# Taking the elementwise work off GpSimd in a two-layer recurrent and convolutional backbone

## The chip, the cores and the metric

The kernel runs on one core of a Trainium2 chip. The metric is the device time of one execution in microseconds. Within the core, TensorE does the matrix products, VectorE, ScalarE and GpSimd the elementwise work, and SyncE (SP) issues the DMAs. The engines run side by side and wait for one another by semaphores; each takes its own instructions strictly in the order of its program. In the profile they are PE (with PEld for its weight loads), DVE, ACT, POOL and SP.

## The reference

Two layers over 1024 latent tokens of 1024 channels, with a context of 256 tokens that goes through the first mixer alone. All is float32. Cut to what is computed:

```python
for l in range(2):
    sm, cm, gm, sf, cf, gf = split(silu(c) @ ada_w[l] + ada_b[l], 6)     # modulation, also of c_ctx
    hl = rms_norm(x, norm_mix_g[l]) * (1 + cm) + sm
    if l == 0:      # bidirectional RG-LRU, the context in front of the latents in each direction
        u = conv(hl @ w_x)                             # width 4, and the same for the context
        r, i = sigmoid(u @ w_r + b_r), sigmoid(u @ w_i + b_i)     # by heads of 256 channels
        a = exp(8 * r * log_sigmoid(lam)); b = sqrt(1 - a * a) * i * u
        h = scan(a, b) forward + scan(a, b) backward
        y = (gelu(hl @ w_gate) * h) @ w_out
    else:           # short gated convolution
        b, g, v = split(hl @ w_in, 3); y = (b * conv3(g * v)) @ w_out
    x = x + gm * y
    hl = rms_norm(x, norm_ffn_g[l]) * (1 + cf) + sf
    g, v = split(hl @ w_up, 2)
    x = x + gf * ((silu(conv3(g)) * v) @ w_down)
return rms_norm(x, final_g)
```

## The kernel before

Channels lie on the 128 partitions, tokens along the free axis, so a tensor of 1024 channels is eight tiles of 128 x 1024. Every product is made of three products in a shorter format: each operand is split into a high part (hi, rounded to fp32r) and a low part (the source minus hi), and hi x hi, hi x lo and lo x hi go into the same PSUM bank (`mm`, line 436). `split` (line 231) makes the parts: the high one on ScalarE, or on the engine that it is given, the low one always on VectorE.

The stages of the first 455 us, around which the change lies, in order:

The start (`start`, line 567). Per tile k of x: load x and a column block of the modulation weights; `dot` (line 314) makes one modulation column as the sum of a row-wise product of 1024 columns (on VectorE one instruction with an accumulator; on GpSimd a product, and then a pass of ScalarE that sums it); the weights scaled by it are split (tiles wh/wl of the code, bh and bl in the trace), x is split (uh, ul), squared by ScalarE and added to a running sum of squares (`add(acc, acc, q, ...)`, line 625; acct in the trace), and TensorE runs 18 products. Then the norm is made, and for the second part of the start (lines 651 to 665, from about 53 us) per tile k another modulation column comes (`late_dot`), x is scaled by VectorE (x<-x,cols,cs), split (bh, bl), and 18 products run for each k. Beside that come columns for the context (`ctx_dot`, against ccb).

Then gates and products of latents and context, the norm of the context (`ctx_rstd`, line 696, sums of squares in cs6), and the small chain of 16 columns that makes the softplus (line 524; sp in the trace).

The recurrence (`ri`, line 779), eight blocks of 128 channels. Per block and direction TensorE makes two gates; ScalarE takes them out of PSUM with tanh (mx<-banks), makes the coefficients (mx<-mx,sp), VectorE multiplies and scans (TENSOR_TENSOR_SCAN), and both directions are added and multiplied with the gate. Seven slots of the tile mx hold what is under way. Between the blocks run products for the inputs u, their split (`u_split`, line 727; uh, ul), and modulation columns for later (acct<-acct,cb). At its end `ysplit` (line 857) splits the result (bh, bl). In this stage the weights' high part (wh<-raw) is made by GpSimd: `weight_hi[0] = G` (line 776) stands until `open_ffn` sets it to None.

The weights come through three tiles raw0 and six half-slots (wh, wl). A slot is free when TensorE has run the unit that last used it, so the instruction that makes wh waits for TensorE. PSUM has four banks that take turns (`bank`).

From about 455 us on come the output projection, the feed-forward part, the second layer; there GpSimd has nothing.

The order of the instructions is made by `Plan` (line 52): all instructions are recorded, then every engine gets its list ahead of time. TensorE keeps the program's order; the others take, by a cost per engine and size (`cost`, line 102), what could run next and is due first for TensorE. In these costs an add of 1024 columns is 1.15 us on VectorE and 2.30 us on GpSimd, a high part of 1024 columns 0.96 us on ScalarE and 1.01 us on GpSimd. `weight_item` (line 325), `block_items` (line 335) and `run_units` (line 369) bring the stream of loads and splits into the units.

Of the kernel before, what the change touches and what calls it, by code (L numbers as in the profile page):

```python
# [15 lines left out]
KD = 8  # L16
# [8 lines left out]
# one column per 128 channels of every per-channel vector  # L25
# [10 lines left out]
# the seven products of a 2 x 2 block product, in the order in which they run: the bank each goes to,  # L36
# whether it starts it, and its operand among the blocks of the inputs
# [3 lines left out]
# the products of the modulation of the context beside each step of the start's second part  # L41
DOTS = (0, 0, 0, 1, 1, 2, 2, 2)
# the units of the first mixer after its start: gates, products of the latents and of the context, blocks of the
# recurrence, and columns of the modulation
ORDER = ("g2 shift g3 norm g4 g5 ctx mx us0 e6 x4 r0 d3 x5 d2 r1 d2 us2 x6 d1 r2 d1 x7 d1 r3 d1 us4 d1 r4 d1 g6 r5 "
         "us6 g7 r6 r7")
# the functions that the table serves which comes with a function
# [4 lines left out]
class Plan:  # L52
    """Records the instructions and gives every engine its order ahead of time. The tensor engine keeps the program's
    order; the others take, among what could run next, the instruction that the tensor engine needs first."""
# [11 lines left out]
    def record(self, engine, op, a, k):  # L66
# [19 lines left out]
        if func:  # L86
            # those that share a table may pass each other
            if TABLE[func] != self.table[0]:
                self.table = TABLE[func], self.table[2], []
            preds.update(self.table[1])  # L90
            self.table[2].append(i)
# [9 lines left out]
    @staticmethod  # L101
    def cost(engine, op, a, k):
        """How long the engine is held"""
        if engine == "sync":
            return 4 * int(np.prod(a[0].shape)) / 360e3
        n = max(int(np.prod(v.shape[1:])) for v in list(a) + list(k.values()) if isinstance(v, bass.AP))
        if engine == "tensor":
            n = a[2].shape[-1]
            return max(n, 128) / 2400 * (4 if a[2].dtype == F32 else 1)
        if engine == "scalar":  # L110
            return 0.09 + n * 0.85e-3 + (0.09 if "accum_out" in k else 0)
        if engine == "gpsimd":
            return 0.15 + n * (2.1e-3 if op == "tensor_tensor" else 0.84e-3)
        return 0.07 + n * (6.25e-3 if op == "reciprocal" else 1.05e-3)

    @staticmethod
    def lag(a, b):
        """From the end of an instruction to the start of one that waits for it"""
        return 0.0 if a == b else 0.95 if a == "sync" else 1.9 if b == "sync" else 0.2

    def flush(self):
# [9 lines left out]
        # the latest start that keeps the tensor engine going  # L131
# [52 lines left out]
def hybrid_kernel(ctx: ExitStack, tc: tile.TileContext, out, xs, cs, c, cc, ada, vecs,  # L184
# [18 lines left out]
    def ring(name, n):  # L203
        """The next of n slots that take turns"""
        turn[name] = turn.get(name, -1) + 1
        return turn[name] % n
# [67 lines left out]
    units = []  # L274
# [11 lines left out]
    class Raw:  # L286
        """A load in the stream into one of the tiles of a pool, and the items that still need it"""
# [3 lines left out]
    class Item:  # L291
        """An entry of the stream: prep(slots, raws) makes the operand that the key stands for"""
# [21 lines left out]
    def dot(dst, raw, bt, eng=None):  # L314
        """dst = the sums of raw * bt along the rows"""
# [19 lines left out]
    def block_items(name, src1, src2, again):  # L335
        """The seven operands that two tiles of weights give: A11 A12 are the halves of the first, A21 A22 those
        of the second"""
# [31 lines left out]
    def run_units(nside):  # L369
        """Emit the units in order. What they need comes ahead as slots allow, with nside(key) modulation chunks  # L370
        behind each weight."""
# [64 lines left out]
    def mm(ps, w, wi, rh, rl, start, stop, **o):  # L436
        """ps += w[:, wi].T @ (rh + rl), both operands in two exact parts"""
# [29 lines left out]
    def norm_quick(acc, n, dg, ps=None, more=None):  # L467
        """1 / sqrt(mean + eps) per token, on all partitions: the sums with the tokens on the partitions, then
        spread from a diagonal (products with ones and zeros)"""
# [17 lines left out]
    # cols: per norm an A (8) and a B (8)  # L487
# [4 lines left out]
    def make_ab(i, src, l, sh, sc, gname, k=None):  # L492
        """A = g (1 + scale), B = shift, from the products of the modulation without its bias (in vec with the 1
        added for the scales)"""
# [23 lines left out]
    # ================= start =================  # L518
    # softplus(-lam): max(-lam, 0) + log1p(exp(-|lam|)), the log1p as 2 atanh(z / (2 + z))
# [23 lines left out]
    # ================= layer 0 mixer: RG-LRU =================  # L543
# [23 lines left out]
    def start():  # L567
        """The first products run as the data arrives, before the norm is known: with A = g (1 + scale),
        z = W.T (A x r + B) = ((A W).T x) r + W.T B"""
        A, B = ab(0)  # L570
        NM = 3
        # memory that is not in use yet
# [23 lines left out]
        # the tensor engine runs at its full clock only when it is kept busy; a bank that is not in use yet  # L596
# [7 lines left out]
        for k in range(KD):  # L604
# [19 lines left out]
            if k:  # L624
                add(acc, acc, q, G if k < 6 else V)
# [16 lines left out]
        # the next three tiles, from the norm itself as it comes  # L642
# [8 lines left out]
        for k in range(KD):  # L651
            late_dot(k, G)
# [43 lines left out]
    def ctx_rstd():  # L696
        acc, r = cs6[:, 0], cs6[:, 1]
        act(acc, xc[:, 0], AF.Square)
        for k in range(1, KD):
            q = cs6[:, 2 + k % 4]  # L700
            act(q, xc[:, k], AF.Square)
            add(acc, q, acc, G)
# [15 lines left out]
    def conv_a(z, u, m):  # L718
        """z (psum) -> u: width 4, two to the left, one to the right"""
# [7 lines left out]
    def u_split(m):  # L727
        uh[m], ul[m] = uht[:, m % 2], ult[:, m % 2]
        split(uh[m][:, ALL], ul[m][:, ALL], u32[m], G)
        split(uh[m][:, CT], ul[m][:, CT], uc[:, m], G)  # L730
# [41 lines left out]
    def open_mx():  # L772
# [3 lines left out]
        weight_hi[0] = G  # L776
        tpool[0] = lambda n: mxp[0][:, ring("mx", NMX), :n]

    def ri(m):
        """Both directions of one block of 128 channels: gates, coefficients and scans"""  # L780
        hd, mo = m // 2, m % 2

        def f(*ws):
            st = []
            # the slots in the order in which the block before lets go of them
# [3 lines left out]
            for d in range(2):  # L789
                q = d * 8 + m  # L790
                # the scan takes the context first: it stands left of the latents forward, right of them backward
# [16 lines left out]
                # sigmoid(z) = (1 + tanh(z / 2)) / 2, the halves of the biases in vec  # L808
# [13 lines left out]
            # 1 - a^2 = tanh(-log(a) / 2) (1 + a)^2  # L822
# [11 lines left out]
            for d, (q, lat, ct, R, il, ic, I) in enumerate(st):  # L834
# [5 lines left out]
                else:  # L840
                    rev = slice(None, None, -1)
                    mul(ic, ic, Tn[:, ct], G)
# [6 lines left out]
            if m in gt:  # L849
                add(fw, fw, bw, G)  # L850
                mul(x[:, m], gt[m], fw)
            else:
                add(x[:, m], fw, bw, G)
# [3 lines left out]
    def ysplit(h, ms):  # L857
        for m in ms:
            split(hhi[m][:, H[h]], hlo[m][:, H[h]], x[:, m, H[h]], G if m < 6 else None)
            load_x(m, H[h])  # L860

    side += [(ada[0, o + k], modc[:, o + k:o + k + 1], ccb, V if o else G) for k in range(KD) for o in (0, 8)]
    mods = [mod_item(0, j) for j in range(16, 48)] + [mod_item(1, j) for j in range(48)]

    def ahead_dots(todo, room=None):
        """Modulation of later parts, as time allows"""
# [44 lines left out]
    def open_ffn():  # L911
# [10 lines left out]
        # where stored inputs land while no sums are in the way  # L922
        more["stage"] = [flat(more["s"], i, 2) for i in (0, 2, 4)]
        # snapshots of sums, sums of weights, and what the norms need
# [7 lines left out]
    def block_norm(i, slots):  # L932
        """slots: 28 in the order in which they come free. The input of the products is A (x r) + B, in halves of
        the channels (first digit) and of the tokens (second); T1 to T4 are the sums that block products take."""
# [30 lines left out]
        def sums():  # L965
            # in the bank that the last of the first four units takes
# [33 lines left out]
    def blocks(name, src1, src2, post, early=False):  # L1000
        """256 output channels for all tokens from the blocks of the norm: seven products of blocks in place of
        eight. post(row, half, a, b) takes a sum a + b, or b alone."""
# [45 lines left out]
    def run_blocks(us, second, n, skip):  # L1048
        """The first four units begin with what needs only the first half of the tokens. n columns of the modulation
        come beside the products"""  # L1050
# [25 lines left out]
    def act_items(l, n, slots, h, afters, load_after, src, direct=()):  # L1076
        """The stored inputs of the next products, two tiles of 128 channels at a time"""
# [19 lines left out]
    # ================= layer 0 mixer, output =================  # L1097
# [7 lines left out]
    def out_proj(i, l, keys, yh, yl, slots, cols_args, early=()):  # L1105
        """early: tiles and halves that go together, the last input of all of them last, as it may come late"""
# [48 lines left out]
    # ================= FFN =================  # L1155
    def ffn(l, second, i):
# [36 lines left out]
        def store_blocks(q, a, b):  # L1193
            """Two tiles as the blocks that the second product takes: tokens in halves, a above b"""
# [19 lines left out]
    def act_item(key, src, load_after, slots, after, pool="raw"):  # L1214
        """A stored input of products, two tiles of 128 channels"""
# [5 lines left out]
    def down(l, ends, i):  # L1221
        """The second product: blocks for the first 16 tiles of its inputs, in two groups, then the
        other six"""
# [53 lines left out]
    def down_blocks(l, g, q, role):  # L1277
        """x += gate * (products of blocks) for 256 channels, each sum as soon as it stands in its bank"""
# [119 lines left out]
def _tiles(w):  # L1398
    """(1024, M) -> (M / 128, 128, 1024): per 128 output channels a tile with the inputs on the partitions"""
# [46 lines left out]
```

## Time and profile before

| | |
|---|---|
| median of three runs | 2135.06 us (2134.78 to 2135.86) |
| span of the profiled execution | 2134.5 us |
| TensorE busy | 2047.5 us, 96%, 9218 products |
| VectorE busy | 1809.7 us, 85%, 2564 instructions |
| ScalarE busy | 1033.5 us, 48%, 1561 instructions |
| GpSimd busy | 173.1 us, 8%, 93 instructions |
| DMA | 307.05 MB, mean 144 GB/s |

A busy share is a mean over stages that differ. The table says of the whole that TensorE has 87 us without work; where they lie, a view by windows tells. An instruction's duration in the trace is the time that it holds its engine, and that can include waiting for something other than a semaphore, which no list of waits shows: to see it, one compares the durations of the same form (same operation, same tiles, same shape) at different times.

### The profile page before, as it was taken

What the parts mean: (1) busy time and instruction counts of PE and PEld (TensorE: products, weight loads), DVE (VectorE), ACT (ScalarE), POOL (GpSimd) and SP (SyncE); (2) the same over time, 40 slices, a digit from 0 to 9 for tenths busy, and PEclk for the clock granted to TensorE, in tenths of its full rate; (3) what the DMA queues carried; (4) which work ended last, traced back from release to release, by engine and by line L of the source; (5) the groups of instructions that cost most, each with busy time, mean ns of one, the idle gap of its engine ahead of it and who ended that gap; (6) DMA issues with size and microseconds to landing.
All of it is one profiled execution on the core that took longest, in us unless ns stands there. A gap on an engine that the chain in (4) does not pass through costs nothing.

```text
span 2134.5 us, 25093 instructions
## 1 busy us (share of the span) xinstructions
PE 2047.5 (96%) x9218; PEld 1689.4 (79%) x9218; DVE 1809.7 (85%) x2564; ACT 1033.5 (48%) x1561; POOL 173.1 (8%) x93
## 2 busy tenths in 40 slices
PE   7789889699999999999999999999999999999998
PEld 5579767588788888878888788888888888888888
DVE  7988899978998989788868988867988878688867
ACT  4564666525654344454335533434654444454345
POOL 4620335310000000000000000000000000000000
PEclk9999989899999999999999999999999999999999
DMA  7455122353233545474354144673233343364345
GB/s 261 159 175 188 40 87 72 99 186 110 89 114 123 178 163 173 157 236 146 114 166 140 54 155 165 222 242 111 71 119 129 122 151 131 109 216 160 127 131 165
DMA packets 103418, 307.05 MB, mean 144 GB/s; under 512 B 10368, under 2 KB 14720, under 8 KB 103168
## 3 DMA queue, kind: packets, MB, share of 16 engines
q1 hardware_dynamic: 103296, 305.46, 43.7%
q8 instruction: 72, 1.18, 0.2%
q14 instruction: 50, 0.41, 0.1%
HBM read 248.80 MB, written 56.62 MB: 143 GB/s over the span
## 4 chain that ended last, share of the span: by engine, by line
PE 82%; DVE 8%; issue 2%; ACT 1%; DMA 0%; POOL 0%; DVEq 0%; ACTq 0%
PE banks L165 82%; DVE mx L165 2%; DVE x L165 2%; DVE bl L165 1%; DVE wl L165 1%; DVE u L165 1%; DVE acct L165 1%; DVE sp L165 0%; DVE ul L165 0%; ACT mx L165 0%; DMA s<-bd 0%; DVE uc L165 0%; DMA acct<-in_ada 0%; ACT wh L165 0%; DVE s L165 0%
## 5 line engine op out<-in xcount | busy, mean ns | idle before, releaser
L165 PE MATMUL banks<-bl,wh 128*128 128x512 f32 (+1 forms) x2720 | 1053.8, 387 | 14.3 <-DVE bl L165 14.2
L165 PE MATMUL banks<-bh,wl 128*128 128x512 f32 (+1 forms) x2720 | 1053.8, 387 | 14.2 <-DVE wl L165 14.1
L165 PE MATMUL banks<-bh,wh 128*128 128x512 f32 (+1 forms) x2720 | 1056.8, 389 | 5.0 <-ACT bh L165 3.0
L165 PEld LDWEIGHTS banks<-bl,wh 128*128 128x128 f32 x2720 | 513.3, 189 | 125.6 <-DVE bl L165 21.8
L165 PEld LDWEIGHTS banks<-bh,wl 128*128 128x128 f32 x2720 | 513.3, 189 | 121.2 <-DVE wl L165 19.3
L165 PEld LDWEIGHTS banks<-bh,wh 128*128 128x128 f32 x2720 | 513.3, 189 | 111.7 <-ACT bh L165 4.7
L165 ACT ACTIVATE wh<-raw 128x512 fp32r<-128x512 f32 (+2 forms) x369 | 258.0, 701 | 472.7 <-PE banks L165 391.8
L165 DVE TENSOR_TENSOR wl<-raw,wh 128x512 fp32r<-128x512 f32 (+2 forms) x386 | 306.7, 803 | 62.0 <-ACT wh L165 58.3
L165 DVE SCALAR_TENSOR_TENSOR x<-banks,mod,x 128x512 f32<-128x512 f32 (+1 forms) x184 | 132.6, 726 | 96.2 <-PE banks L165 95.2
L165 ACT ACTIVATE s<-banks 128x512 f32<-128x512 f32 x174 | 103.7, 596 | 195.2 <-PE banks L165 192.0
L165 ACT ACTIVATE wh<-s 128x512 fp32r<-128x512 f32 x216 | 135.5, 628 | 110.5 <-DVE s L165 63.8
L165 DVE TENSOR_TENSOR wl<-s,wh 128x512 fp32r<-128x512 f32 x216 | 148.6, 689 | 39.2 <-ACT wh L165 35.4
L165 DVE TENSOR_TENSOR s<-s,banks 128x512 f32<-128x512 f32 x158 | 107.9, 684 | 37.4 <-PE banks L165 37.1
L165 DVE SCALAR_TENSOR_TENSOR x<-s,vec,x 128x504 f32<-128x504 f32 x132 | 96.4, 740 | 10.2 <-ACT x L165 9.0
L165 PE MATMUL banks<-uh,wh 128*128 128x512 f32 (+1 forms) x192 | 72.6, 378 | 26.4 <-ACT mx L165 17.6
L165 DVE SCALAR_TENSOR_TENSOR acct<-acct,cb 128x1024 f32<-128x1024 f32 x69 | 89.6, 1299 | 4.0 <-DMA acct<-in_ada 3.9
L165 PE MATMUL banks<-ul,wh 128*128 128x512 f32 (+1 forms) x192 | 71.8, 374 | 5.0 <-DVE ul L165 5.0
L165 PE MATMUL banks<-uh,wl 128*128 128x512 f32 (+1 forms) x192 | 71.0, 370 | 0.0
L165 ACT ACTIVATE mx<-mx,sp 128x1280 f32<-128x1280 f32 x32 | 45.9, 1455 | 44.6 <-DVE x L165 27.6
L165 ACT ACTIVATE bh<-s 128x512 fp32r<-128x512 f32 x88 | 51.5, 624 | 32.6 <-DMA s<-bd 31.3
L165 PEld LDWEIGHTS banks<-uh,wh 128*128 128x128 f32 x192 | 38.7, 202 | 34.2 <-ACT mx L165 20.4
L165 ACT ACTIVATE mx<-banks,vec 128x1024 f32<-128x1024 f32 (+1 forms) x64 | 47.0, 792 | 38.6 <-DVE mx L165 24.3
(167 smaller groups left out, 1945.9 us busy)
## 6 DMA issues: line engine op xcount, KB each, us to landing
raw<-in_wup SPq DMA_DIRECT2D x92, 512.0 KB, 3.6
acct<-in_ada SPq DMA_DIRECT2D x69, 512.0 KB, 3.5
bd<-x SPq DMA_DIRECT2D x48, 512.0 KB, 3.2
s<-bd SPq DMA_DIRECT2D x44, 512.0 KB, 4.3
raw<-in_wdn SPq DMA_DIRECT2D x32, 512.0 KB, 4.2
raw<-in_wdn SPq DMA_DIRECT2D x40, 384.0 KB, 3.3
raw<-in_wbi SPq DMA_DIRECT2D x26, 512.0 KB, 4.1
u<-in_ada SPq DMA_DIRECT2D x24, 512.0 KB, 4.5
```

What stands on the lines that cost most here:

```text
L165: getattr(getattr(self.tc.nc, e), op)(*a, **k)
```

## The change

Every elementwise instruction that the program puts on GpSimd goes elsewhere. To VectorE: the adds of the sums of squares (latents and context), the modulation columns that GpSimd made (there as one instruction with an accumulator, so that ScalarE's second pass falls away), the product of 256 columns in the backward direction of each block, and the sum of the two directions. To ScalarE: the high parts of weights (in the recurrence), of u and of the mixer's result. The order of all engines is made anew by the planner. Nothing else differs (the diff also takes out the comments, not shown).

```diff
@@ start
             if k:
-                add(acc, acc, q, G if k < 6 else V)
+                add(acc, acc, q)
@@
         for k in range(KD):
-            late_dot(k, G)
+            late_dot(k, V)
@@ ctx_rstd
-            add(acc, q, acc, G)
+            add(acc, q, acc)
@@ u_split
-        split(uh[m][:, ALL], ul[m][:, ALL], u32[m], G)
-        split(uh[m][:, CT], ul[m][:, CT], uc[:, m], G)
+        split(uh[m][:, ALL], ul[m][:, ALL], u32[m])
+        split(uh[m][:, CT], ul[m][:, CT], uc[:, m])
@@ open_mx
-        weight_hi[0] = G
@@ ri
-                    mul(ic, ic, Tn[:, ct], G)
+                    mul(ic, ic, Tn[:, ct])
@@
             if m in gt:
-                add(fw, fw, bw, G)
+                add(fw, fw, bw)
                 mul(x[:, m], gt[m], fw)
             else:
-                add(x[:, m], fw, bw, G)
+                add(x[:, m], fw, bw)
@@ ysplit
-            split(hhi[m][:, H[h]], hlo[m][:, H[h]], x[:, m, H[h]], G if m < 6 else None)
+            split(hhi[m][:, H[h]], hlo[m][:, H[h]], x[:, m, H[h]])
@@
-    side += [(ada[0, o + k], modc[:, o + k:o + k + 1], ccb, V if o else G) for k in range(KD) for o in (0, 8)]
+    side += [(ada[0, o + k], modc[:, o + k:o + k + 1], ccb, V) for k in range(KD) for o in (0, 8)]
```

## Rows read from the trace of the kernel before

**Rows 1.** Windows: stretch, length, busy us of PE, PEld, DVE, ACT, POOL; clock, DMA.
```profile
15.00:53.30 38.30, 27.56 (x103) 20.16 (x101) 34.60 (x29) 14.51 (x17) 22.47 (x8) 0.91 0.65 238
53.30:116.00 62.70, 47.49 (x177) 34.20 (x178) 61.66 (x67) 32.83 (x52) 32.41 (x10) 0.92 0.47 161
116.00:150.00 34.00, 28.31 (x121) 22.95 (x120) 26.83 (x41) 22.09 (x31) 12.29 (x10) 0.90 0.53 178
150.00:228.00 78.00, 78.00 (x446) 68.96 (x445) 64.48 (x95) 42.90 (x50) 5.92 (x5) 1.00 0.47 158
228.00:455.00 227.00, 187.72 (x848) 154.91 (x847) 219.56 (x179) 129.73 (x129) 99.17 (x56) 0.92 0.25 80
455.00:2134.50 1679.50, 1666.11 (x7474) 1377.18 (x7472) 1395.69 (x2141) 782.29 (x1271) 0.05 (x1) 1.00 0.45 147
```
**Rows 2.** TensorE's waits, 15 to 455 us: total us, times, longest.
```profile
PE banks L165 <- ACT mx L165: 17.6, 3, 6.3
PE banks L165 <- DVE wl L165: 13.9, 4, 6.7
```
**Rows 3.** Timeline of the start, VectorE and GpSimd: start us, us, instruction.
```profile
10.47 1.23 DVE L165 SCALAR_TENSOR_TENSOR u<-u,cb 128x1024 f32<-128x1024 f32 x1
...
18.52 0.22 DVE L165 SCALAR_TENSOR_TENSOR cols<-mod,vec 128x1 f32<-128x1 f32 x1
...
20.48 2.95 POOL L165 TENSOR_TENSOR acct<-acct,uc 128x1024 f32<-128x1024 f32 x1 [3.09 <-ACT uc L165]
21.09 3.42 DVE L165 SCALAR_TENSOR_TENSOR u<-u,cb 128x1024 f32<-128x1024 f32 x1
...
42.68 2.17 DVE L165 SCALAR_TENSOR_TENSOR cols<-mod,vec 128x1 f32<-128x1 f32 x1
...
50.83 1.21 DVE L165 TENSOR_TENSOR acct<-acct,uc 128x1024 f32<-128x1024 f32 x1
```
**Rows 4.** Groups by form, VectorE, 15 to 53.3 us: count, busy, mean ns, idle before.
```profile
L165 DVE SCALAR_TENSOR_TENSOR u<-u,cb 128x1024 f32<-128x1024 f32 x6 | 18.3, 3057 | 0.0
```
**Rows 5.** Groups by form, VectorE, 53.3 to 116 us.
```profile
L165 DVE SCALAR_TENSOR_TENSOR x<-x,cols,cs 128x512 f32<-128x512 f32 x16 | 18.0, 1143 | 0.0
L165 DVE SCALAR_TENSOR_TENSOR bl<-x,cols,bh 128x512 fp32r<-128x512 f32 x16 | 13.5, 873 | 0.3
L165 DVE TENSOR_TENSOR cols<-mod,vec 128x1 f32<-128x1 f32 x8 | 12.1, 1515 | 0.0
L165 DVE SCALAR_TENSOR_TENSOR u<-u,ccb 128x1024 f32<-128x1024 f32 x4 | 7.0, 1751 | 0.0
```
**Rows 6.** Timeline, VectorE, 97.4 to 98.2 us, with GpSimd silent.
```profile
97.44 0.74 DVE L165 SCALAR_TENSOR_TENSOR x<-x,cols,cs 128x512 f32<-128x512 f32 x1
98.11 0.15 DVE L165 TENSOR_TENSOR cols<-mod,vec 128x1 f32<-128x1 f32 x1
```
**Rows 7.** Groups by form, VectorE, 116 to 150 us: the softplus.
```profile
L165 DVE TENSOR_TENSOR sp<-sp 128x16 f32<-128x16 f32 x9 | 6.0, 662 | 0.3
L165 DVE TENSOR_SCALAR sp<-sp 128x16 f32<-128x16 f32 x10 | 3.5, 362 | 3.7 <-ACT sp L165 3.4
...
L165 DVE SCALAR_TENSOR_TENSOR sp<-sp 128x16 f32<-128x16 f32 x1 | 0.2, 176 | 0.0
```
**Rows 8.** Groups by form, VectorE, from 455 us to the end.
```profile
L165 DVE SCALAR_TENSOR_TENSOR acct<-acct,cb 128x1024 f32<-128x1024 f32 x56 | 68.3, 1219 | 3.7 <-DMA acct<-in_ada 3.6
```
**Rows 9.** Timeline, VectorE: first and last stretched instructions of the recurrence.
```profile
235.83 1.53 DVE L165 TENSOR_TENSOR_SCAN mx<-mx,uc 128x256 f32<-128x256 f32 x1
...
452.51 3.61 DVE L165 TENSOR_TENSOR wl<-raw,wh 128x1024 fp32r<-128x1024 f32 x2
```
**Rows 10.** Groups by form, GpSimd, 228 to 455 us.
```profile
L165 POOL TENSOR_SCALAR wh<-raw 128x1024 fp32r<-128x1024 f32 x16 | 26.1, 1639 | 43.7 <-PE banks L165 41.2 <-issue 2.5
```
**Rows 11.** Groups by form, ScalarE, up to 455 us: prices of a high part.
```profile
L165 ACT ACTIVATE wh<-raw 128x1024 fp32r<-128x1024 f32 x18 | 19.0, 1054 | 18.7 <-PE banks L165 12.3 <-DMA raw<-in_wg 4.8 <-ACT uc L165 0.9
...
L165 ACT ACTIVATE bh<-x 128x512 fp32r<-128x512 f32 x4 | 2.3, 620 | 12.0 <-DVE x L165 12.0
```

## The prediction

> **What bounds the kernel now.** I read the windows first, one per stage [rows 1]. From 455 us to the end TensorE is busy 1666.1 of 1679.5 us and GpSimd ends one instruction there and does nothing more, so the change moves nothing in it; from 150 to 228 us TensorE is busy for all 78.0 us. What can move lies in four other stretches, in which TensorE stands idle: the start, 15 to 53.3 us (38.3 - 27.6 = 10.7 us idle), its second part to 116 us (62.7 - 47.5 = 15.2), the stretch to 150 us (5.7), and the blocks of the recurrence, 228 to 455 us (227.0 - 187.7 = 39.3). Together 70.9 us: the most that any change of these stages gives back, but for the clock, which the same rows show at 0.90 to 0.92 in all four. In the same rows VectorE is busy 61.7 of 62.7 us and 219.6 of 227.0 us. The waits of TensorE [rows 2] name ScalarE's tile mx and VectorE's wl as what comes last most; mx is slots and evictions that ScalarE in turn gets late from VectorE. So the bound of these stages is VectorE.
>
> Then I asked why VectorE is full, and the timeline of the start tells it [rows 3]. The dot product of 1024 columns takes 1.23 us at 10.47 and 3.42 us at 21.09. GpSimd's add ran from 20.48 to 23.43; 23.43 plus the 1.2 us of the dot is 24.6, and the dot ended at 24.51. It did no work until GpSimd's instruction was through. Laid side by side, the VectorE instructions ahead of 460 us that are stretched by over 0.15 us against the shortest of their form each overlap one of GpSimd, without exception; what they hold above it comes to 86 us (the four reliefs below). After 455 us, where GpSimd is silent, the mean of 56 dots is 1.22 us [rows 8].
>
> **The change, part by part.** The sum is made against the span of 2134.5 us; the median of the runs is 0.6 us above it, and I add that at the end. No moved instruction issues a DMA; SP's and GpSimd's queues are not passed. Every moved instruction is in the planner's lists, so the order of all engines is made anew.
>
> 1. Start to 53.3 us. Six dots take 18.3 us together, a mean of 3.06 [rows 4], five of them beside GpSimd's adds, and 6 x 1.23 = 7.4 if free: 11.0 us with rounding. From 42.68 on three instructions (cols, bl, ul) take 8.15 us up to 50.83, where the same three take 2.57 from 18.52 to 21.09: 5.6 us [rows 3]. Relief 16.6. Added on VectorE: five adds at the 1.21 us of the add at 50.83, 6.1. Net gain 10.5, just what TensorE has idle there. Three dots that GpSimd took early (41 to 50 us) are not due before the second part; I count them there. If the planner puts them here, 3.9 us less here. The bounds are thus 6.6 and 10.7.
>
> 2. To 116 us. Above their free times stand eight cols (the add of one column that follows a dot), 8 x (1.515 - 0.15) = 10.9; sixteen x, 16 x (1.143 - 0.74) = 6.4; sixteen bl at the same 0.74, 16 x (0.873 - 0.74) = 2.1; four dots with ccb, 4 x (1.751 - 1.23) = 2.1 [rows 5, 6]. Relief 21.5. Added: ten dots of this stretch and three of the one before at 1.23 + 0.07 for reading the accumulator (an estimate of 1.3 in all), 16.9. Net gain 4.6. ScalarE loses the second pass of each, which hides today. Nothing hides the dots: VectorE is full here. Some have no product waiting soon and can go on to 150 us, where VectorE is idle for 13.5 of 78 us; by that the gain goes up to the 15.2 that TensorE has idle. I stay at 4.6, since the tiles they load into take turns and four of the eight context dots must go ahead of later ones.
>
> 3. To 150 us. The short chain of the softplus waits behind GpSimd: nine products at 0.662 and ten scalings at 0.362 us against 0.176 for one that is free [rows 7], 4.4 + 1.9 = 6.3 us. Behind it on VectorE stands a wl for which TensorE idles. Moved here: seven adds of 256 columns (at most 0.5 each by the line through 0.74 at 512 and 1.21 at 1024 columns, an estimate) and three dots, 3.5 + 3.9 = 7.4 us, against 34.0 - 26.8 = 7.2 us in which VectorE idles [rows 1]. Hidden, I say; if that cover is gone, the stage gains nothing. Between 0 and 5.7, I take 5, nearer to the idle row, since the dots are due later than the chain.
>
> 4. 228 to 455 us. Fifty stretched instructions, the first and the last in [rows 9], hold 41.7 us above their free times. Added on VectorE: eight adds of 1024 at 1.21 and eight products of 256 at 0.5, 9.7 + 4.0 = 13.7. VectorE's bound: gain 28.0, the stretch then 199. ScalarE takes sixteen wh at 1.05, twelve bh at 0.62, six uh of 1024 at 1.05 and six of 256 at 0.40 (the line through the two others, an estimate) [rows 11]: 16.8 + 7.4 + 6.3 + 2.4 = 32.9, so 162.6 busy in place of 129.7 [rows 1]. And a wh waits until TensorE lets go of its slot: GpSimd stood 41.2 us in those waits [rows 10], which cost nothing as nothing was queued behind. On ScalarE the tanh evictions are queued behind, and TensorE waits for their banks. If all of it adds, ScalarE needs 162.6 + 41.2 = 203.8 us: a gain of 23. I take this end, the nearer to the rows; the other is 39.3, TensorE's idle time.
>
> Sum: 10.5 + 4.6 + 5 + 23 = 43.1; 2134.5 - 43.1 + 0.6 = 2092.
>
> **A rule against the change.** Rows first: VectorE is 97% busy from 228 to 455 us and 98% from 53.3 to 116 us [rows 1], and the change gives it 36.7 us more. [...]
>
> **Rivals.** (a) The stretching was never GpSimd's doing, but of something that runs at the same times (DMA, TensorE's reads). VectorE then keeps its 86 us and takes 6.1 + 16.9 + 13.7 = 36.7 us more in full stages: 2135 + 36.7 = 2172. It makes the kernel slower from the point where less than 36.7 of the 86 us goes away. Against it: no stretched instruction without GpSimd beside it, and ends that fall at GpSimd's end plus the instruction's own time. (b) ScalarE becomes the bound of the recurrence: each of the eight blocks loses 2.3 to 3.4 us more, as a wh that waits holds back evictions that could run: 18 to 27 us, the whole at 2110 to 2119. To end slower than before it would have to be 43 / 8 = 5.4 us a block. For it: 80% busy in 204 us, and table loads between. Against it: the wh waits and the evictions follow the same order of products. (c) VectorE ceases to be the bound: all TensorE idle goes, 70.9 us, or 2064; for it speaks that GpSimd's 3 us steps also leave the chains (the add at the end of each block takes 1.21 on VectorE); against it, VectorE's 199 us of work in the last stage against TensorE's 188. (d) The change doesn't do what it says, an operation stays on GpSimd or the planner undoes it: 2130 to 2139. The diff leaves no user of G, so little.
>
> **How the numbers follow.** Chances: the forecast, 2080 to 2108, 0.60; (c) below 2080, 0.17; (b) 2108 to 2130, 0.15; (d) 0.03; (a) 0.05. 0.2% of this kernel is about 4 us, what a measurement tells from no change. Faster 0.60 + 0.17 + 0.15 = 0.92, same 0.03, slower 0.05. The range for 8 in 10 takes most of (b) and of (c): 2068 to 2116.
>
> **What would show it.** Right, if GpSimd has but its memsets left; if the dots of the start take 1.2 us throughout; if VectorE's forms have one duration throughout; if TensorE's idle time in the recurrence falls from 39 to about 16 us with ScalarE near 163 us busy. If ScalarE waits there for TensorE in front of wh, and TensorE for mx as much as before, step 4 was too good. The forecast is wrong as a whole if the long instructions stay long with GpSimd silent.

## The result and the profile after

The changed kernel takes 2080.26 us (median; 2077.5 to 2082.59) against 2134.92 us (2134.15 to 2135.86): a ratio of 0.9744, with a 95% interval of 0.973 to 0.9758. That is 54.7 us less, where 43 were forecast. The profiled execution, the longest of the four, has a span of 2080.8 us.

The windows of the kernel after come first, one per stage, cut where TensorE has done as many products as at the cuts of [rows 1]. The columns are those of [rows 1].

```profile
15.00:41.30 26.30, 23.77 (x104) 18.72 (x102) 23.64 (x34) 17.78 (x20) 0.00 (x0) 1.00 0.94 367
41.30:95.30 54.00, 45.29 (x178) 31.48 (x179) 51.76 (x86) 16.49 (x23) 0.00 (x0) 0.97 0.53 167
95.30:127.30 32.00, 29.56 (x120) 24.18 (x119) 29.07 (x47) 21.19 (x27) 0.00 (x0) 0.89 0.64 213
127.30:205.20 77.90, 77.90 (x447) 68.91 (x446) 66.66 (x110) 45.41 (x55) 0.00 (x0) 1.00 0.44 155
205.20:402.60 197.40, 182.95 (x849) 151.51 (x848) 192.16 (x195) 155.56 (x167) 0.00 (x0) 0.97 0.28 93
402.60:2080.80 1678.20, 1664.90 (x7473) 1375.65 (x7471) 1394.39 (x2141) 783.79 (x1274) 0.00 (x0) 1.00 0.45 147
```

Against [rows 1] the lengths fall by 12.0, 8.7, 2.0, 0.1, 29.6 and 1.3 us: 53.7, all of it (2134.5 - 2080.8). Two columns share each gain. TensorE's idle time (length less PE busy) goes from 10.7 to 2.5, 15.2 to 8.7, 5.7 to 2.4 and 39.3 to 14.5 us in the four stages that could move: 42.8 us together. And the same products take less busy time, 27.56 to 23.77, 47.49 to 45.29 and 187.72 to 182.95 us, in the three of these stages in which the granted clock rose; in the third it fell by 0.01 and they take 1.25 us more. Together that is 9.5 us. The last 1.4 us are those of the other two stages.

In the recurrence VectorE is still busy 192.16 of 197.4 us, more than any other engine. Its instructions are what changed. Below are groups by form on VectorE after the change, the first two of the recurrence (205 to 402.6 us), the others of the start's second part (41.3 to 95.3 us):

```profile
L165 DVE SCALAR_TENSOR_TENSOR acct<-acct,cb 128x1024 f32<-128x1024 f32 x12 | 14.6, 1217 | 0.0
L165 DVE SCALAR_TENSOR_TENSOR mx<-mx,u 128x1024 f32<-128x1024 f32 x5 | 6.1, 1217 | 0.0
...
L165 DVE SCALAR_TENSOR_TENSOR x<-x,cols,cs 128x512 f32<-128x512 f32 x16 | 11.9, 746 | 1.0 <-ACT cs L165 1.0
L165 DVE SCALAR_TENSOR_TENSOR bl<-x,cols,bh 128x512 fp32r<-128x512 f32 x16 | 11.6, 748 | 0.5
L165 DVE SCALAR_TENSOR_TENSOR u<-u,cb 128x1024 f32<-128x1024 f32 x9 | 11.0, 1219 | 0.0
L165 DVE SCALAR_TENSOR_TENSOR u<-u,ccb 128x1024 f32<-128x1024 f32 x8 | 9.8, 1220 | 0.0
L165 DVE TENSOR_TENSOR cols<-mod,vec 128x1 f32<-128x1 f32 x8 | 1.2, 152 | 0.0
```

The first two forms took these times in the recurrence of the kernel before (228 to 455 us):

```profile
L165 DVE SCALAR_TENSOR_TENSOR acct<-acct,cb 128x1024 f32<-128x1024 f32 x12 | 20.1, 1679 | 0.3 <-DMA acct<-in_ada 0.3
L165 DVE SCALAR_TENSOR_TENSOR mx<-mx,u 128x1024 f32<-128x1024 f32 x5 | 11.3, 2251 | 0.0
```

The dot product has the 1.22 us of [rows 8] in every stage, the x and bl of [rows 5] have 0.75, and the one-column add went from 1.515 us to 0.152. No VectorE instruction is stretched by 0.15 us any more. The start's timeline shows the same: one step of it is now 3.8 us, from a dot at 15.12 us to the next at 18.95, without one of 3.42 us as in [rows 3].

```profile
15.12 1.22 DVE L165 SCALAR_TENSOR_TENSOR u<-u,cb 128x1024 f32<-128x1024 f32 x1
16.27 0.08 DVE L165 DVE_READ_ACCUMULATOR u<-u,cb 128x1 f32 x1
16.38 0.22 DVE L165 SCALAR_TENSOR_TENSOR cols<-mod,vec 128x1 f32<-128x1 f32 x1
...
18.95 1.22 DVE L165 SCALAR_TENSOR_TENSOR u<-u,cb 128x1024 f32<-128x1024 f32 x1
```

What TensorE still waits for from 15 to 402.6 us (total us, times, longest), against [rows 2]:

```profile
PE banks L165 <- DVE bl L165: 7.6, 11, 1.2
PE banks L165 <- ACT mx L165: 7.0, 2, 4.3
PE banks L165 <- DVE ul L165: 3.1, 1, 3.1
PE banks L165 <- DVE u L165: 2.7, 2, 2.4
```

The wait for mx fell from 17.6 to 7.0 us. The 13.9 us for wl of [rows 2] are no longer among the long ones.

### The profile page after: what moved, and what is told of

Same layout as the page of the kernel before. It is cut to its first block, busy times and chain, and to the rows that moved or that the text cites. A ratio compares the mean times of both kernels' runs of the same rounds, so it can differ in the third digit from the quotient of the medians.

```text
span 2080.8 us, 25029 instructions
## 1 busy us (share of the span) xinstructions
PE 2036.8 (98%) x9218; PEld 1681.5 (81%) x9218; DVE 1764.5 (85%) x2624; ACT 1049.3 (50%) x1574; POOL 0.2 (0%) x4
## 4 chain that ended last, share of the span: by engine, by line
PE 84%; DVE 9%; ACT 4%; DMA 2%; issue 1%; SPq 0%; DVEq 0%; ACTq 0%
PE banks L165 84%; ACT mx L165 2%; DVE x L165 2%; DVE mx L165 2%; DVE u L165 2%; DVE bl L165 2%; DMA x<-in_xs 1%; DVE wl L165 1%; DMA s<-bd 1%; ACT L165 1%; ACT bh L165 1%; DMA raw<-in_wg 0%; DVE uc L165 0%; DVE ul L165 0%; DVE acct L165 0%
## 5 line engine op out<-in xcount | busy, mean ns | idle before, releaser
L165 PE MATMUL banks<-bl,wh 128*128 128x512 f32 (+1 forms) x2720 | 1052.2, 387 | 11.0 <-DVE bl L165 10.9
L165 ACT ACTIVATE wh<-raw 128x512 fp32r<-128x512 f32 (+2 forms) x386 | 275.6, 717 | 475.0 <-PE banks L165 394.7
L165 DVE SCALAR_TENSOR_TENSOR acct<-acct,cb 128x1024 f32<-128x1024 f32 x69 | 84.1, 1218 | 4.5 <-DMA acct<-in_ada 4.5
L165 ACT ACTIVATE bh<-s 128x512 fp32r<-128x512 f32 x88 | 51.5, 624 | 35.3 <-DMA s<-bd 34.0
L165 ACT ACTIVATE bh<-x,cols 128x512 fp32r<-128x512 f32 x64 | 45.1, 721 | 42.1 <-DVE cols L165 27.3
L165 DVE TENSOR_TENSOR x<-x,s 128x512 f32<-128x512 f32 x90 | 61.0, 686 | 0.8
L165 DVE TENSOR_TENSOR bl<-s,bh 128x512 fp32r<-128x512 f32 x88 | 57.2, 684 | 5.0 <-ACT bh L165 5.0
```

The source lines that it names most:

```text
L165: getattr(getattr(self.tc.nc, e), op)(*a, **k)
```

## The experiments

Theory: a GpSimd instruction that reads SBUF holds up a VectorE instruction with two SBUF inputs (the on-chip memory in which the tiles lie), so the 86 us were GpSimd's doing and went with it. Rivals: the stretching has another cause (a); ScalarE's waits with wh limit the recurrence (b); VectorE is no longer the bound (c).

**GpSimd reading beside the changed kernel.** Nothing that is computed needs the added work; it only keeps GpSimd busy in the recurrence, in place of what was taken away. The line on VectorE makes it start there.

```diff
 def open_mx():
     nc.flush()
     cpx.close()
+    tc.nc.vector.tensor_tensor(out=eye[:, :1], in0=eye[:, :1], in1=eye[:, :1], op=ALU.max)
+    for _ in range(200):
+        tc.nc.gpsimd.tensor_tensor(out=eye, in0=eye, in1=eye, op=ALU.mult)
```

> The changed kernel with 200 products of 128 columns added on GpSimd that nobody waits for, from the first block of the recurrence on (a tile of zeros and ones times itself, which stays what it is). Theory (GpSimd's reading holds up VectorE instructions with two inputs): GpSimd is busy for some 100 us as in the kernel before (99 us there), the two-input forms of VectorE in that stretch grow by 0.1 to 0.5 us each, and with VectorE busy 97% there the time goes from 2080 to 2095 to 2115 us. Rival (the gain came from shorter chains and a new order, the long durations were incidental): the order of VectorE, ScalarE and TensorE is that of the changed kernel, so the time stays at 2080 within 4 us and the forms keep their durations.

Measured: 2101.18 us (ratio to the kernel before 0.9843, 0.9828 to 0.9857), 20.9 us over the changed kernel. The added products run from 171 to 389 us; GpSimd is busy for 202 us with them, twice what was expected. The groups by form of this run, GpSimd in the whole run and VectorE from 205 to 390 us:

```profile
L777 POOL TENSOR_TENSOR eye<-eye 128x128 f32<-128x128 f32 x200 | 202.1, 1011 | 186.3 <-DVE eye L775 170.7
```

```profile
L165 DVE SCALAR_TENSOR_TENSOR acct<-acct,cb 128x1024 f32<-128x1024 f32 x12 | 17.0, 1417 | 0.0
...
L165 DVE SCALAR_TENSOR_TENSOR u<-banks,vec,u 128x1023 f32<-128x1023 f32 x4 | 5.1, 1277 | 0.1
L165 DVE TENSOR_TENSOR ul<-uc,uh 128x256 fp32r<-128x256 f32 x6 | 3.6, 616 | 0.0
```

A dot (two inputs from SBUF) takes 1417 ns in place of 1217, and ul of 256 columns 616 in place of 418: 0.2 us each, at 256 columns as at 1024. The form that reads a PSUM bank (banks) keeps its 1.28 us. ScalarE's wh stays at 1.05 us. So the stretching comes back with GpSimd's reads, on VectorE instructions with two SBUF inputs. Rival (a) falls.

VectorE instructions with a single input tensor, from SBUF, don't occur in this stretch, so the run says nothing of them. The kernel before does: three scalings of the softplus (one input, 16 columns; part of the 0.362 us of [rows 7]) took 1.20, 0.60 and 0.60 us beside GpSimd, and the others 0.17. The first of them, with the GpSimd instruction that it overlaps:

```profile
133.41 2.40 POOL L165 TENSOR_TENSOR raw<-raw,ccb 128x1024 f32<-128x1024 f32 x1
...
134.64 1.20 DVE L165 TENSOR_SCALAR sp<-sp 128x16 f32<-128x16 f32 x1 [3.42 <-ACT sp L165]
```

Not every form with one input is held up: the RECIPROCAL behind it took 0.25 us beside GpSimd, as it does alone.

**GpSimd writing only.** The same with 400 memsets in place of the 200 products, and one DMA that loads eye again.

```diff
+    for _ in range(400):
+        tc.nc.gpsimd.memset(eye, 0.0)
 ...
 def open_ffn():
     nc.flush()
+    tc.nc.sync.dma_start(eye, ident)
```

> The 400 memsets again, with the load that restores their tile issued only at the end of the recurrence, so that it doesn't stand in SP's queue ahead of the weights' loads (in the kernel before this one it stood there for 101.9 us). Writes without reads don't hold up VectorE: 2080 us within 4, two-input forms at 1.22 us for 1024 columns. If GpSimd's writes cost something that the durations don't show: over 2086.

Measured: 2079.55 us (0.9738, 0.9724 to 0.9753), the time of the changed kernel. Groups by form, GpSimd in the whole run and VectorE from 175 to 290 us (the memsets run from 172 to 277 us):

```profile
L777 POOL MEMSET eye<- 128x128 f32 x400 | 81.9, 205 | 194.3 <-DVE eye L775 171.3
```

```profile
L165 DVE SCALAR_TENSOR_TENSOR acct<-acct,cb 128x1024 f32<-128x1024 f32 x7 | 8.5, 1218 | 0.0
```

82 us of GpSimd's writes cost VectorE nothing, in the dot as in the other two-input forms of that stretch. For these it is reading that counts.

A first form of this experiment had the reload recorded one line earlier, ahead of the flush.

> The changed kernel with 400 memsets of 128 columns added on GpSimd at the same place, which read nothing (the tile is loaded again behind them). If the inputs of GpSimd are what collides with VectorE's second input, nothing grows: 2080 us within 4, the two-input forms at 1.22 us for 1024 columns. If any activity of GpSimd holds up VectorE, it costs as much as the reads do for the same busy time.

It took 2137.63 us, for a reason of its own: the reload stood in SP's queue ahead of the loads that the recurrence needs. The waits of SP, and its timeline:

```profile
SPq L165 <- POOL eye L777: 101.9, 1, 101.9
```

```profile
173.02 0.77 SPq L165 DMA_DIRECT2D acct<-in_ada  x1
275.77 0.33 SPq L165 DMA_DIRECT2D eye<-in_ident  x1
276.20 0.38 SPq L165 DMA_DIRECT2D raw<-in_wri  x1
```

SP issues nothing for 102 us. It says nothing of what GpSimd does to VectorE, but it prices one DMA that waits in the wrong place: 58 us against 2079.55.

**One half of the change.** v_part moves the sums of squares, dots and products to VectorE, and leaves the high parts on GpSimd; s_part does the reverse. Against the changed kernel, v_part is

```diff
-        split(uh[m][:, ALL], ul[m][:, ALL], u32[m])
-        split(uh[m][:, CT], ul[m][:, CT], uc[:, m])
+        split(uh[m][:, ALL], ul[m][:, ALL], u32[m], G)
+        split(uh[m][:, CT], ul[m][:, CT], uc[:, m], G)
...
+        weight_hi[0] = G
...
-            split(hhi[m][:, H[h]], hlo[m][:, H[h]], x[:, m, H[h]])
+            split(hhi[m][:, H[h]], hlo[m][:, H[h]], x[:, m, H[h]], G if m < 6 else None)
```

> One part alone: sums, dots and the sum of directions on VectorE, the high parts stay on GpSimd as before. Theory (relief of VectorE less what it takes): the start gains its whole 23 us; in the recurrence GpSimd keeps 62 of its 99 us, so about 16 of the 42 us of stretching go and 13.7 are added, a gain of 2: 2110 us (2104 to 2116). Rival (GpSimd's 3 us steps in the chains were the cost, its splits harmless): nearly all of the gain, 2090 or less.

and s_part gives the argument G back to the five sums and products and to the dots:

```diff
-                add(acc, acc, q)
+                add(acc, acc, q, G if k < 6 else V)
...
-            late_dot(k, V)
+            late_dot(k, G)
...
-                    mul(ic, ic, Tn[:, ct])
+                    mul(ic, ic, Tn[:, ct], G)
...
-                add(fw, fw, bw)
+                add(fw, fw, bw, G)
```

> The other part alone: high parts on ScalarE, sums, dots and products stay on GpSimd. Theory: the start gains nothing; in the recurrence 26 of the 42 us of stretching go and VectorE takes nothing: 2109 us (2103 to 2117). Rival (ScalarE loses as much by waiting in front of the weights as VectorE wins): 2125 to 2140.

Measured: 2099.37 us (0.9836, 0.982 to 0.9853) and 2115.7 us (0.9911, 0.9896 to 0.9926). The gains against the runs of before beside them (2134.63) are 35.3 and 18.9 us, together 54.2; the whole change gives 54.7. The halves add up. v_part lies between what was expected (2104 to 2116) and its rival (2090 or less), s_part inside its range. The recurrence of v_part, then of s_part: each time its window (columns as above), and under it two of VectorE's groups by form:

```profile
202.60:419.00 216.40, 188.66 (x849) 154.78 (x848) 211.30 (x194) 129.56 (x128) 61.37 (x40) 0.94 0.25 85
```

```profile
L165 DVE SCALAR_TENSOR_TENSOR acct<-acct,cb 128x1024 f32<-128x1024 f32 x12 | 15.4, 1285 | 0.0
...
L165 DVE SCALAR_TENSOR_TENSOR mx<-mx,u 128x1024 f32<-128x1024 f32 x5 | 6.1, 1217 | 0.0
```

```profile
226.80:436.10 209.30, 186.99 (x848) 153.39 (x847) 198.12 (x180) 155.81 (x167) 36.06 (x16) 0.94 0.26 87
```

```profile
L165 DVE SCALAR_TENSOR_TENSOR acct<-acct,cb 128x1024 f32<-128x1024 f32 x12 | 18.9, 1577 | 0.0
...
L165 DVE SCALAR_TENSOR_TENSOR mx<-mx,u 128x1024 f32<-128x1024 f32 x5 | 10.5, 2096 | 0.0
```

The start gains all of its share in v_part (the recurrence begins at 202.6 us, as early as with the whole change) and none in s_part (226.8). In the recurrence the whole 29.6 us are 10.6 of v_part and 17.7 of s_part. The expectations had put nearly all of it on s_part (26 us) and 2 us on v_part, since they shared out the stretching by GpSimd's busy time. Form by form, against the means of the changed kernel, what is left of it in VectorE is 20.2 us with 61.4 us of GpSimd's splits (0.33 us per us) and 17.7 us with 36.1 us of its adds and products (0.49 per us). By busy time it would have been 26 and 16 us, so this accounts for two thirds of the miss of v_part, and for about a quarter of that of s_part: there VectorE's busy time fell by 21.4 us and the recurrence by 17.7. The adds read two tensors and take 3.6 us each in s_part, the splits read one; mx<-mx,u stays at 2.1 us in s_part and is free in v_part. Whether the second input or the length makes the adds dearer is not shown.

**The high parts of the weights alone back to GpSimd.** This is the test of rival (b): on GpSimd, wh waits for its slot where it holds back nothing.

```diff
+        weight_hi[0] = G
```

> The changed kernel with the high part of the recurrence's weights alone back on GpSimd (17 instructions). The prediction's step 4 charged ScalarE with the 41.2 us that these instructions waited for TensorE. If that charge is real, this kernel is faster than the changed one: below 2076. If not (the planner puts them where the slot is free), what counts is that GpSimd reads again for 27 us beside VectorE: 17 instructions that hold up VectorE by some 0.5 to 1 us each, 2086 to 2096.

Measured: 2089.15 us (0.9781, 0.9767 to 0.9796), 9 us over the changed kernel; the recurrence takes 205.2 us with 23.5 us of GpSimd in it, in place of 197.4, and VectorE is busy for 200.8 us of it in place of 192.2. Below is wh on ScalarE in the changed kernel (205 to 402.6 us), which answers [rows 10]:

```profile
L165 ACT ACTIVATE wh<-raw 128x1024 fp32r<-128x1024 f32 x16 | 16.7, 1055 | 2.4 <-PE banks L165 2.4
```

ScalarE waits 2.4 us for slots, not the 41.2 that GpSimd stood there. Rival (b) falls: wh on ScalarE is the better place.

**Columns taken out of the recurrence.** This tests whether VectorE's work is what is left there, and whether a faster kernel follows. ORDER keeps 13 columns of the modulation (a d each, 1.3 us of VectorE) among the blocks; early_cols moves nine of them ahead, early_all all.

```diff
-ORDER = "... g4 g5 ctx mx us0 e6 x4 r0 d3 x5 d2 r1 d2 us2 x6 d1 r2 d1 x7 d1 r3 d1 us4 d1 r4 d1 ..."
+ORDER = "... g4 g5 d5 ctx d4 mx us0 e6 x4 r0 x5 r1 us2 x6 r2 x7 d1 r3 d1 us4 d1 r4 d1 ..."      # early_cols
+ORDER = "... g4 g5 d5 ctx d8 mx us0 e6 x4 r0 x5 r1 us2 x6 r2 x7 r3 us4 r4 ..."                 # early_all
```

> The changed kernel, with nine of the thirteen modulation columns that the units of the recurrence carry placed ahead of it, in the stretch that TensorE fills alone and in which VectorE idles for 11 us. Theory (VectorE's work still sets the recurrence: 192 of 197 us): nine dots at 1.24 us leave it, 2069 to 2075. Rival (chains between ScalarE and VectorE set it): 2078 to 2084.

> The same with all thirteen placed ahead. If VectorE's work sets the recurrence and the stretch before takes all of it: 2064 to 2072. If VectorE has no room left there (11 us idle, 16 us of dots), the last ones delay the first block: no better than nine.

Measured: 2103.68 us (0.9851, 0.9834 to 0.9867) and 2116.79 us (0.9911, 0.9896 to 0.9925), both slower than the changed kernel. The timeline of early_cols ahead of the recurrence:

```profile
182.82 1.23 DVE L165 SCALAR_TENSOR_TENSOR acct<-acct,cb 128x1024 f32<-128x1024 f32 x1 [3.41 <-DMA acct<-in_ada]
...
187.54 1.23 DVE L165 SCALAR_TENSOR_TENSOR acct<-acct,cb 128x1024 f32<-128x1024 f32 x1 [3.49 <-DMA acct<-in_ada]
...
204.68 0.80 PE L165 MATMUL banks<-ul,wh 128*128 128x512 f32 x1 [26.17 <-DVE ul L165]
```

All the columns go through the one tile acct, so each dot waits 3.5 us for a load that could not start before the dot ahead of it, and an ul that TensorE needs stands behind them: 26 us. The recurrence itself got 4.6 us shorter (for the same 847 products 192.8 in place of 197.4 us). With all thirteen out it is 192.3 us, with VectorE busy for 180.6 and TensorE for 180.0. The expectation of a faster kernel missed on the load's tile; but the work bought less than was expected, too: 11.5 us less of VectorE gave 5.2.

So early_rooms takes six columns ahead, each into one of three tiles that are free after the context's norm; ORDER keeps the seven others.

```diff
+            rooms = [xcf[:, :D], xcf[:, D:], csf2[:, :D]]      # halves of xc, and of cs6
...
+                if m < 6:
+                    call(ahead_dots, [mods.pop(0)], lambda m=m: rooms[m % 3])
```

> Six of the thirteen columns ahead of the recurrence, but loaded in turn into three tiles that are free after the norm of the context, in place of one. In early_cols the nine columns through one tile took 26 us of waiting for their loads, which ended ahead of the recurrence, while the recurrence itself became 4.8 us shorter. Theory (the loss there was that row of loads): with three tiles VectorE's idle time ahead of the recurrence takes the six dots, and the recurrence gets 3 to 4 us shorter: 2074 to 2079. Rival (the planner puts them last whatever the tiles): a wait of 5 to 15 us in front of the recurrence, 2084 to 2094.

Measured, with the changed kernel again beside it:

> The changed kernel itself beside it on the same chip, as the measure for a difference of a few us: 2080 within 4.

2078.82 us (0.974, 0.9727 to 0.9753) against 2079.77 us (0.9747, 0.9734 to 0.9761). The 1 us between them is not told apart. The recurrence of early_rooms:

```profile
205.20:400.00 194.80, 181.79 (x851) 151.00 (x850) 186.53 (x182) 156.22 (x167) 0.00 (x0) 0.97 0.23 77
```

It is about 3 us shorter for 5.6 us less of VectorE (192.16 to 186.53), and some 1 us was lost ahead of it. VectorE's work thus still counts there, at about half its price. The other way it costs nearly all of it: in dummy_read VectorE is busy 23.2 us longer in the recurrence, which takes 21.3 us more. So VectorE's work bounds the recurrence up to about where the changed kernel stands; below that, the rival of early_cols (chains between ScalarE and VectorE) has its part, which no run isolates.

## Why the prediction was right, and where it was off

The forecast of 2092 us was 12 us too high. 2080.26 lies in the range for 8 in 10, and at the very edge between the forecast's 2080 to 2108 and rival (c)'s below 2080.

**The bound and the mechanism** were right. VectorE was full of waiting that the profile counts as its busy time; with GpSimd silent every form has one duration, within 0.15 us, and GpSimd's reads bring the waiting back. Its busy time ahead of the last stage fell by 43.8 us (407.13 to 363.29, from the windows); the steps gave 86 - 36.7 - 7.4 = 41.9. What the runs show of the waiting: beside GpSimd's reads in dummy_read the forms with two SBUF inputs take up to 0.2 us more (the dot 1417 ns in place of 1217), beside its memsets nothing (1218 ns in dummy_write2), and the form that reads a bank takes 1277 ns beside reads and 1281 without. On one input the kernel before shows both sides, the scalings at up to 1.20 us and the RECIPROCAL at 0.25; what sets the two apart, no run shows, nor by what means one engine holds up the other.

**What the sum left out: the clock.** The steps counted TensorE's idle time, and the idle time fell by 42.8 us where 43.1 were forecast. That the total agrees so well is partly luck, as the steps below show. The gain was larger by the 9.5 us in which the same products ran faster. Where slow products stand is to be seen in the kernel before, behind TensorE's longest wait for mx (timeline of TensorE):

```profile
266.33 0.76 PE L165 MATMUL banks<-uh,wh 128*128 128x512 f32 x1 [6.34 <-ACT mx L165]
266.89 0.63 PE L165 MATMUL banks<-ul,wh 128*128 128x512 f32 x1
...
270.02 0.39 PE L165 MATMUL banks<-uh,wh 128*128 128x512 f32 x1
```

After 6.34 us of idling the first products take 0.63 us each, one every 0.43 us, at a mean granted clock of 0.54; from 270 us on they take 0.39, one every 0.23, at 1.00. Windows of the same stretch (length, PE busy, granted clock, DMA share, GB/s):

```profile
262.00:266.00 4.00, 0.00 (x0) 0.61 0.00 0
266.00:270.00 4.00, 3.67 (x9) 0.54 0.41 120
270.00:274.00 4.00, 4.00 (x21) 1.00 0.03 11
```

This stretch was paid for twice: once as idle time, and once in the nine products behind it, which took 3.7 us in place of 9 x 0.23 = 2.1. From 262 to 266 us, within the idling, the clock already averages 0.61; that the idling lowers it is the author's reading, which no run isolates. The granted clock of the recurrence rose from 0.92 to 0.97, and its products took 4.8 us less. The 0.90 to 0.92 of [rows 1] stood in the prediction, named as an exception to the bound and put into no term.

Two limits go with the 9.5 us. The clock differs between executions: in the stage to 127.3 us the changed kernel's profile has a clock of 0.89, and that of dummy_read, where VectorE and ScalarE have the same order up to there, has 1.00, with 2.8 us of idle time in it (29.40 - 26.61) against 2.4 (its window of that stage, columns as in [rows 1]):

```profile
95.00:124.40 29.40, 26.61 (x120) 21.54 (x119) 26.95 (x41) 20.90 (x27) 0.00 (x0) 1.00 0.64 212
```

So that stage's clock is not the change's doing. And idle and busy time of TensorE are two columns of one length: in the recurrence VectorE's bound alone gave 28.0 of the 29.6 us, so there no run shows the clock as a gain of its own.

**Step 1** forecast 10.5 us and measured 12.0: 8.2 of idle time and 3.8 of clock (0.91 to 1.00). The relief was right in kind (VectorE is busy for 23.6 us, where 34.6 - 10.5 = 24.1 follow from the step), and all seven sums of squares of this stretch run on VectorE; the clock made up for the 2.3 us of idle time that the step had counted and that stayed. The 16 DMA engines, 65% busy here before, are now 94% busy.

**Step 2** forecast 4.6 and measured 8.7: 6.5 of idle time and 2.2 of clock. The mis-sized term is the thirteen dots. VectorE has 17 of 1024 columns in this stretch and had six, so eleven came; seven of the context's (raw<-raw,ccb) stand in the next stretch, as the upper bound of the step had allowed. The reliefs held: cols 10.9, x 6.1, bl 1.9 us.

**Step 3** forecast 5 and measured 2.0. The idle time fell by 3.2 us, to one wait of 2.44 for VectorE's u, and the products took 1.25 us more at a clock of 0.89. With the clock of 1.00 that dummy_read had there, the stage is some 2.5 us shorter, a gain of about 4.5; in idle time, which is all that the step counted, it is 3.2 of 5. The softplus is not what held: most of its chain moved into the next stage (two of nine products are left here, at 0.17 us). In its place stand the seven dots of step 2 and the seven adds: of the cover of 7.2 us, 2.9 are left (29.07 of 32.0 us busy), and the idle time given back lies between the step's two bounds. One of the dots (107.34 to 108.56 us) stands right ahead of that u. TensorE's timeline there (the only idle time of the stage), and the dots among VectorE's groups by form:

```profile
109.91 1.41 PE L165 MATMUL banks<-ones,cs 128*128 128x1 f32 x6 [2.44 <-DVE u L165]
```

```profile
L165 DVE SCALAR_TENSOR_TENSOR raw<-raw,ccb 128x1024 f32<-128x1024 f32 x7 | 8.4, 1218 | 0.0
```

**Step 4** forecast 23 and measured 29.6: 24.8 of idle time and 4.8 of clock. Of its two bounds it took the wrong one. VectorE's, 199 us, is what came (197.4; VectorE busy 192.16, where relief and added work give 191.6). ScalarE's, 203.8, was made of 162.6 busy, measured 155.6, and 41.2 of waits with wh, measured 2.4. A wait that GpSimd stood because it had nothing else to do was not a price that ScalarE paid: in its new order the instructions come when their slots are nearly free.

**The rivals.** (a) fell by the added reads, and by the changed kernel itself, in which GpSimd is silent and nothing is stretched. (b) fell by wh_gpsimd. (c) holds in the start, where TensorE idles 2.5 of 26.3 us, and not in the recurrence, where VectorE is 97% busy and TensorE idles 14.5 us. (d) fell: GpSimd ran nothing but four memsets. What was weighed against the change, that a VectorE 97 and 98% busy gets 36.7 us more, did not decide it: VectorE took that work and is busy for 43.8 us less ahead of the last stage.

**Left open:** what would take away the 14.5 us that TensorE still idles in the recurrence. Half of it (7.0 us) ends with mx of ScalarE, most of the rest with ul, wl and bl of VectorE; 5.6 us less of VectorE's work gave only 3, and 11.5 us less gave 5.2.

## What to carry to other kernels

Compare one form's duration across stages before calling an engine full: where it is longer beside another engine's work than alone, its busy time holds a wait that no list of waits shows. Weigh GpSimd work by what its reads take from VectorE (here 0.3 to 0.5 us for each us of the kernel's own work, and 0.13 for the short products of dummy_read) and not by its own duration, which looks free. And look behind TensorE's idle time for slow products (here nine that took 3.7 us in place of 2.1), in more than one execution.

## What was not expected of the hardware

What a VectorE instruction loses doesn't go by its own size: the add of one column took 1.515 us on average before [rows 5] and 0.152 after, and beside the added products a form of 256 columns lost the same 0.2 us as one of 1024. GpSimd's own durations spread as well: its 128 x 128 product in dummy_read, always the same work, takes from 0.40 to 2.80 us, with a median of 1.26, and its wh in the kernel before takes 1.06 us at 203.68, where VectorE stands idle, and 2.02 at 360.78, beside VectorE's ul. Nor is the waiting confined to two inputs: scalings of 16 columns with one input, 0.17 us alone, took up to 1.20 us beside GpSimd in the kernel before.
